# One-hot rows of the gates built for four tokens in four instructions, and six PSUM banks for the first product with the experts

## The chip, the core and the metric

The kernel runs on one core of one Trainium2 chip. The metric is the device time of one execution in microseconds (us). Before the change it is 3218.7 us, the median of 3 runs (3213.13 to 3223.79).

## What is computed

Two small networks stand one behind the other over 256 tokens of width 1024. The first has two layers, each a mixer (retention, then a gated spatial unit) followed by a layer of 16384 experts; the second has forgetting attention, a gated delta rule and two convolutional feed-forward layers. The change touches the expert layer alone, which runs twice:

```python
def peer_ffn(h, w_query, sub_keys, expert_u, expert_v):
    q = (ht @ w_query).reshape(T, Hh, 2, PEER_HALF)
    scores = jnp.einsum('thpd,hpkd->thpk', q, sub_keys)
    s_top, i_top = lax.top_k(scores, K)
    cand = (s_top[:, :, 0, :, None] + s_top[:, :, 1, None, :]).reshape(T, Hh, K * K)
    cand_idx = (i_top[:, :, 0, :, None] * PEER_NKEYS + i_top[:, :, 1, None, :]).reshape(T, Hh, K * K)
    best, pos = lax.top_k(cand, K)
    expert_idx = jnp.take_along_axis(cand_idx, pos, axis=-1)
    gates = jax.nn.softmax(best, axis=-1)
...
        a = jax.nn.gelu(jnp.einsum('tkd,td->tk', u, xb)) * g
        return jnp.einsum('tk,tkd->td', a, expert_v[idx])
```

Each token picks 128 experts (8 heads of 16), each named by two indices below 128.

## The kernel before

The kernel gathers nothing. It multiplies all 16384 experts with all tokens, and puts the choice into a dense table of gates, 128 x 128 x 256, in which the experts that a token did not pick are zero. `peer` (line 976) therefore has these stages in each layer: the query projection; the **first product** (loop from line 1016), 128 blocks of 128 experts, each 24 matmuls of 256 columns (`mm3`, lines 402 to 404: three matmuls for one product, because every f32 weight is split into two parts, `whi` and `wlo`); and the second product (`mult`), which multiplies the activated first product by the gates and the second expert table.

Weights come by DMA on SP's queue as `stage` tiles of 16 blocks (1 MB, two buffers), enough for two blocks of experts. `Weights.load` (line 120) splits four blocks at a time, a piece: ScalarE writes `whi` (line 143), then VectorE, or GpSimd for some pieces, subtracts to get `wlo` (line 145). A block of experts needs two pieces. GpSimd takes every second piece while the experts are being picked (`RELIEF`), and every fourth (`RELIEF_G`) once the gates are being built. Up to eight pieces can wait for TensorE in the first of these stretches and four in the second.

After a block's 24 matmuls ScalarE evicts its PSUM bank with a Gelu (line 1023); after every second block the pair goes to DRAM (line 1025, `spill`). These blocks use two PSUM banks in turn, `b0` and `b1` (`begin_banks(2)`, `bank`). `long_bank` gives the two banks `s0` and `s1` to other work, and the second product keeps `b2` to `b5`.

Beside the first product runs `choose` (line 861), a generator that `step` advances between blocks by an account of estimated nanoseconds. It finds the 16 best keys, the 16 best pairs and the softmax, all on VectorE; at lines 931 to 940 it turns places into indices with long bf16 instructions. Then comes the **gate stage** (lines 959 to 973), four tokens at a time, 64 groups. For each token t, `oh` holds three rows of 128 per slot (slots lie on the partitions): a one-hot row of the first index (line 965), and a one-hot row of the second index times the gate, twice, for the gate's f16 value and for its rest (line 967). The rows of 128 key numbers that they are compared with are `line`. Eight matmuls of 128 columns (line 970) turn these into the 128 x 128 gates of four tokens, and ScalarE copies them out (line 972). `oh` has two buffers. VectorE makes 12 instructions for a group.

The order on each engine is that of the program, except where a scheduler moves an instruction ahead of one that it expects to wait. On ScalarE it puts the splitting of weights ahead: the eviction of a block stands behind `whi` of the block four further on, as long as eight pieces can wait, and behind that of the block two further on in the gate stage.

Of the kernel before, what the change touches and what calls it, by code (L numbers as in the profile page):

```python
# [14 lines left out]
HF = mybir.dt.float16  # L15
# [3 lines left out]
ALU = mybir.AluOpType  # L19
# [4 lines left out]
P = 128  # L24
D = 1024
KC = D // P
T = 256
# [25 lines left out]
NK = 128  # L53
# [268 lines left out]
class Kernel:  # L322
# [538 lines left out]
    def choose(self, scores, big, work, chosen, closing):  # L861

        nc = self.nc
        s16 = big.tile([P, 2, 16, TOPK], F32, tag="s16", name="s16")
        ix = big.tile([P, 2, 16, TOPK], U32, tag="ix", name="ix")
        i12 = chosen.tile([P, 2, T], HF, tag="i12", name="i12")
        gp = chosen.tile([P, 2, T], HF, tag="gp", name="gp")
# [7 lines left out]
            nc.vector.tensor_copy(gp[:, 0, ts], tp[:, 2 * P:3 * P])  # L875
            nc.vector.tensor_tensor(gp[:, 1, ts], tp[:, 2 * P:3 * P], gp[:, 0, ts], op=ALU.subtract)

        line = chosen.tile([P, NK], HF, tag="line", name="line")
        self.tc.keep_in_program_order(nc.vector.tensor_copy(line, self.const("iota")))
        for m in range(16):  # L880
            while m not in scores:
                yield -1
# [6 lines left out]
        iota = big.tile([P, TOPK, P], BF, tag="iota16", name="iota16")  # L889
# [3 lines left out]
        for t in range(2):  # L893
# [34 lines left out]
            for u in range(2):  # L928
# [4 lines left out]
                    op=ALU.is_equal)  # L933
                yield 1200
                nc.vector.tensor_tensor(eq, eq, ixb[:, t, u, :, None].to_broadcast([P, TOPK, TOPK, PEER_H]),
                                        op=ALU.mult)
# [22 lines left out]
        for t4 in range(T // 4):  # L959
            ts = slice(4 * t4, 4 * t4 + 4)  # L960
            acc = self.long_bank()
            oh = chosen.tile([P, 4, 3, NK], HF, tag="oh", name="oh", bufs=2)
            for u in range(4):
                t = slice(4 * t4 + u, 4 * t4 + u + 1)
                nc.vector.tensor_scalar(oh[:, u, 0], line, i12[:, 0, t], None, op0=ALU.is_equal)  # L965
                for w in range(2):
                    nc.vector.tensor_scalar(oh[:, u, 1 + w], line, i12[:, 1, t], gp[:, w, t], op0=ALU.is_equal,  # L967
                                            op1=ALU.mult)
                for w in range(2):
                    nc.tensor.matmul(acc[:, u * P:(u + 1) * P], oh[:, u, 0], oh[:, u, 1 + w], start=w == 0,  # L970
                                     stop=w == 1, skip_group_check=True)
            nc.scalar.activation(gates[:, :, ts], acc.rearrange("p (t i) -> p i t", t=4), AF.Copy,
                                 scale=1.0 / GATE_SCALE)
            yield 1400

    def peer(self, layer, later=()):
        nc = self.nc
        with ExitStack() as ctx:
            io = self.pool("peerio", bufs=2, ctx=ctx)
            chosen = self.pool("peersel", ctx=ctx)  # L980
# [27 lines left out]
            w = self.stream(f"peer_query{layer}", KC * 16)  # L1008
# [4 lines left out]
            self.rate = US  # L1013

            w = Weights(self, self.ins[f"peer_u{layer}"], NK * KC)
            for i in range(NK):
                acc = self.bank()[:, :T]
                for k in range(KC):
                    self.mm3(acc, w.tile(i * KC + k), (self.hi[:, k, :T], self.lo[:, k, :T]), k == 0, k == KC - 1)
                self.tick()  # L1020
                if i % 2 == 0:
                    gs = io.tile([P, 2 * T], F32, tag="gs", name="gs").rearrange("p (a b) -> p a b", a=2)
                nc.scalar.activation(gs[:, i % 2], acc, AF.Gelu_apprx_tanh)  # L1023
                if i % 2:
                    nc.scalar.dma_start(spill[i // 2], gs)
                self.step(self.rate)
# [4 lines left out]
            w = Weights(self, self.ins[f"peer_v{layer}"], NK * KC)  # L1031
# [4 lines left out]
            ts = slice(META, L) if layer else slice(0, T)  # L1036
# [6 lines left out]
            for i in range(NK):  # L1043
                if i % 2 == 0:

                    a = (io if i else chosen).tile([P, 2 * T], F32, tag="gs" if i else "oh", name="gs", bufs=2)
                    a = a.rearrange("p (a b) -> p a b", a=2)
# [679 lines left out]
```

## Time and profile before

| | before |
|---|---|
| median of 3 runs | 3218.7 us |
| the profiled execution, its own time | 3223.57 us |
| its span in the trace | 3221.8 us |
| TensorE busy | 3081.6 us (96%) |
| VectorE busy | 2410.0 us (75%) |
| ScalarE busy | 1774.3 us (55%) |
| GpSimd busy | 526.2 us (16%) |
[...]

The profile lists, for one execution, what every engine did and what it waited for. A matmul's recorded duration is its latency, and successive matmuls overlap, so a short pause of TensorE hides inside the busy time; the distance between events that recur once per block of experts is the better measure of its pace. `PEld` is the loading of weights into TensorE, which runs ahead of the matmuls.

### The profile page before, as it was taken

To read this page: it belongs to the slowest core of one execution; us is meant where nothing else is said; L and a number is where in the kernel's file an instruction comes from. 1 tells how busy PE (TensorE), PEld (TensorE's weight loads), DVE (VectorE), ACT (ScalarE), POOL (GpSimd) and SP (SyncE) were. 2 spreads that over 40 slices of the span, in tenths; PEclk is the share of its full clock that TensorE was granted. 3 is DMA by queue.
4 is the path that set the end of the run, shared out by engine and by line. 5 is a ranking of instruction groups with operands and counts; after the bars stand their busy time and mean duration, and the time that the engine had idled before them with its cause. 6 is when DMAs were issued, how large, how long until landed. Compare 5 with 4: busy or idle time off the path is not lost. (4 is left out here: it accounts for less than half of the span.)

```text
span 3221.8 us, 63744 instructions
## 1 busy us (share of the span) xinstructions
PE 3081.6 (96%) x24317; PEld 2932.2 (91%) x24317; DVE 2410.0 (75%) x5694; ACT 1774.3 (55%) x3495; POOL 526.2 (16%) x476
## 2 busy tenths in 40 slices
PE   6999999999999999999999999999999998999998
PEld 5899999999999978999999999999677998898898
DVE  7777979996777687678899877666556965744783
ACT  4566555555555455555555555556456656824763
POOL 1213431110000003234321200000001001133101
PEclk8999999999999999999999999999899999989999
DMA  6655555558777765455555576665323543310453
GB/s 256 243 189 180 198 196 193 187 182 283 260 260 266 269 229 210 157 179 211 188 193 186 203 277 232 234 231 182 110 76 106 197 171 134 118 40 28 145 191 110
DMA packets 119779, 604.14 MB, mean 188 GB/s; under 512 B 14136, under 2 KB 15336, under 8 KB 61488
## 3 DMA queue, kind: packets, MB, share of 16 engines
q1 hardware_dynamic: 98496, 556.84, 48.8%
q10 hardware_dynamic: 19008, 35.72, 3.0%
q0 software_dynamic: 1968, 7.51, 0.7%
q8 instruction: 190, 3.11, 0.4%
q14 instruction: 117, 0.96, 0.1%
HBM read 565.38 MB, written 34.64 MB: 186 GB/s over the span
## 5 line engine op out<-in xcount | busy, mean ns | idle before, releaser
L402 PE MATMUL bank<-hi,whi 128*128 128x256 f32 (+1 forms) x5968 | 1725.4, 289 | 42.0 <-ACT gs L1023 17.5
L404 PE MATMUL bank<-hi,wlo 128*128 128x256 f32 (+1 forms) x5968 | 1707.5, 286 | 32.5 <-DVE wlo L145 30.2
L403 PE MATMUL bank<-lo,whi 128*128 128x256 f32 (+1 forms) x5968 | 1699.3, 285 | 1.2 <-DVE lo L379 1.2
L143 ACT CAST whi<-stage 128x512 fp32r<-128x512 f32 x1780 | 1077.0, 620 | 1051.7 <-PE bank L403 740.5
L145 DVE TENSOR_TENSOR wlo<-stage,whi 128x512 fp32r<-128x512 f32 x1566 | 1084.6, 707 | 468.0 <-ACT whi L143 452.1
L402 PEld LDWEIGHTS bank<-hi,whi 128*128 128x128 f32 x5968 | 1140.5, 191 | 62.1 <-ACT gs L1023 19.0
L404 PEld LDWEIGHTS bank<-hi,wlo 128*128 128x128 f32 x5968 | 1138.0, 191 | 52.2 <-DVE wlo L145 48.8
L403 PEld LDWEIGHTS bank<-lo,whi 128*128 128x128 f32 x5968 | 1139.0, 191 | 4.9 <-DVE lo L379 2.2
L145 POOL TENSOR_TENSOR wlo<-stage,whi 128x512 fp32r<-128x512 f32 x214 | 306.3, 1433 | 725.0 <-ACT whi L143 717.7
L967 DVE TENSOR_SCALAR oh<-line,i,gp 128x128 f16<-128x128 f16 x1024 | 337.5, 372 | 0.0
L403 PE MATMUL bank<-zl,whi 128*128 128x272 f32 (+1 forms) x736 | 211.3, 287 | 1.0 <-DVE zl L379 1.0
L402 PE MATMUL bank<-zh,whi 128*128 128x272 f32 (+1 forms) x736 | 211.7, 288 | 0.0
L404 PE MATMUL bank<-zh,wlo 128*128 128x272 f32 (+1 forms) x736 | 211.2, 287 | 0.0
L965 DVE TENSOR_SCALAR oh<-line,i 128x128 f16<-128x128 f16 x512 | 150.8, 295 | 0.0
L185 POOL TENSOR_TENSOR sqa<-sqa,sq 128x272 f32<-128x272 f32 (+1 forms) x36 | 30.0, 834 | 692.3 <-ACT sq L183 692.3
L403 PEld LDWEIGHTS bank<-zl,whi 128*128 128x128 f32 x736 | 140.2, 190 | 1.8 <-DVE zl L379 1.4
L402 PEld LDWEIGHTS bank<-zh,whi 128*128 128x128 f32 x736 | 140.1, 190 | 0.7 <-issue 0.4
L404 PEld LDWEIGHTS bank<-zh,wlo 128*128 128x128 f32 x736 | 139.8, 190 | 0.2 <-issue 0.2
L1049 DVE TENSOR_TENSOR gs<-gs,gates 128x512 f32<-128x512 f32 x128 | 88.1, 688 | 55.8 <-DMA gs<-spill 55.5
L1023 ACT ACTIVATE gs<-bank 128x256 f32<-128x256 f32 x256 | 96.8, 378 | 8.0 <-PE bank L404 7.9
L379 DVE TENSOR_TENSOR lo<-gs,hi 128x512 fp32r<-128x512 f32 x126 | 86.4, 686 | 0.4
L378 ACT CAST hi<-gs 128x512 fp32r<-128x512 f32 x126 | 77.9, 618 | 15.1 <-DVE gs L1049 15.0
(432 smaller groups left out, 3114.8 us busy)
## 6 DMA issues: line engine op xcount, KB each, us to landing
stage<-in_peer_u SPq DMA_DIRECT2D x128, 1024.0 KB, 4.8
stage<-in_peer_v SPq DMA_DIRECT2D x128, 1024.0 KB, 5.0
adaw<-in_ada_w SPq DMA_DIRECT2D x96, 512.0 KB, 4.9
stage<-in_ffn_up SPq DMA_DIRECT2D x44, 1024.0 KB, 4.8
spill<-gs ACTq DMA_DIRECT2D x128, 256.0 KB, 2.0
gs<-spill SPq DMA_DIRECT2D x128, 256.0 KB, 5.0
stage<-in_ffn_down SPq DMA_DIRECT2D x22, 1024.0 KB, 4.7
stage<-in_peer_query SPq DMA_DIRECT2D x16, 1024.0 KB, 4.8
```

The costliest lines, as they stand in the source:

```text
L143: k.nc.scalar.copy(hi, src)
L145: eng.tensor_tensor(lo, src, hi.bitcast(F32), op=ALU.subtract)
L185: k.nc.gpsimd.tensor_tensor(self.sum, self.sum, sq, op=ALU.add)
L378: self.nc.scalar.copy(hi, src)
L379: self.nc.vector.tensor_tensor(lo, src, hi.bitcast(F32), op=ALU.subtract)
L402: mm(acc, wh, xh, start=first, stop=False, skip_group_check=True)
L403: mm(acc, wh, xl, start=False, stop=False, skip_group_check=True)
L404: mm(acc, wl, xh, start=False, stop=last, skip_group_check=True)
L965: nc.vector.tensor_scalar(oh[:, u, 0], line, i12[:, 0, t], None, op0=ALU.is_equal)
L967: nc.vector.tensor_scalar(oh[:, u, 1 + w], line, i12[:, 1, t], gp[:, w, t], op0=ALU.is_equal, op1=ALU.mult)
L1023: nc.scalar.activation(gs[:, i % 2], acc, AF.Gelu_apprx_tanh)
L1049: nc.vector.tensor_tensor(a, a, self.gates[:, i:i + 2], op=ALU.mult)
```

## The change

The three rows of a token are no longer made token by token. The key numbers are written twice each (`rep`: 0 0 1 1 2 2 ...), and one instruction makes a kind of row for four tokens as two pairs, the two tokens of a pair interleaved: element 2k+b belongs to key k and token b. So there is one comparison for the first index, one for the second, and two multiplications of the latter with the two parts of the gate: four instructions of 512 elements in place of twelve of 128. All four have two tensor operands. The matmuls stay, eight for a group, but read every second f16 of their rows, as weights and as moving operand. `oh` has a fourth row kind; its tile and its two buffers stay in the same place. The first product takes banks `b0` to `b5` in turn, save for the last four blocks, which stay with `b0` and `b1`.

```diff
-        line = chosen.tile([P, NK], HF, tag="line", name="line")
-        self.tc.keep_in_program_order(nc.vector.tensor_copy(line, self.const("iota")))
+        rep = chosen.tile([P, NK, 2], HF, tag="rep", name="rep")
+        self.tc.keep_in_program_order(
+            nc.vector.tensor_copy(rep, self.const("iota")[:, :, None].to_broadcast([P, NK, 2])))
...
-            oh = chosen.tile([P, 4, 3, NK], HF, tag="oh", name="oh", bufs=2)
-            for u in range(4):
-                t = slice(4 * t4 + u, 4 * t4 + u + 1)
-                nc.vector.tensor_scalar(oh[:, u, 0], line, i12[:, 0, t], None, op0=ALU.is_equal)
-                for w in range(2):
-                    nc.vector.tensor_scalar(oh[:, u, 1 + w], line, i12[:, 1, t], gp[:, w, t], op0=ALU.is_equal,
-                                            op1=ALU.mult)
-                for w in range(2):
-                    nc.tensor.matmul(acc[:, u * P:(u + 1) * P], oh[:, u, 0], oh[:, u, 1 + w], start=w == 0,
-                                     stop=w == 1, skip_group_check=True)
+            oh = chosen.tile([P, 4, 2, NK, 2], HF, tag="oh", name="oh", bufs=2)
+            pairs = lambda a: a[:, ts].rearrange("p (a b) -> p a b", b=2)[:, :, None, :].to_broadcast([P, 2, NK, 2])
+            both = rep[:, None].to_broadcast([P, 2, NK, 2])
+            nc.vector.tensor_tensor(oh[:, 0], pairs(i12[:, 0]), both, op=ALU.is_equal)
+            nc.vector.tensor_tensor(oh[:, 3], pairs(i12[:, 1]), both, op=ALU.is_equal)
+            for w in range(2):
+                nc.vector.tensor_tensor(oh[:, 1 + w], oh[:, 3], pairs(gp[:, w]), op=ALU.mult)
+            for u, w in itertools.product(range(4), range(2)):
+                nc.tensor.matmul(acc[:, u * P:(u + 1) * P], oh[:, 0, u // 2, :, u % 2], oh[:, 1 + w, u // 2, :, u % 2],
+                                 start=w == 0, stop=w == 1, skip_group_check=True)
...
+            wide = itertools.cycle(f"b{i}" for i in range(6))
             for i in range(NK):
-                acc = self.bank()[:, :T]
+                acc = (self.bank() if i >= NK - 4 else self.bank(next(wide)))[:, :T]
```

On TensorE, ScalarE, GpSimd and SP every instruction keeps its place; only PSUM banks and line numbers differ. On VectorE the rows of the gates are replaced, and near the end of the picking a few neighbours change places. VectorE in the middle of the gate stage of layer 0, before (numbers tell the tiles apart; `DVE`, `PE`, `Activation` behind "waits" are VectorE itself, TensorE and ScalarE; `wlo` is the split of a piece of weights):

```order
L965 TENSOR_SCALAR oh_6226<-line_3070,i12_3068 128x128 [waits PE_49]
L967 TENSOR_SCALAR oh_6226<-line_3070,i12_3068,gp_3069 128x128 x2
L965 TENSOR_SCALAR oh_6226<-line_3070,i12_3068 128x128
L967 TENSOR_SCALAR oh_6226<-line_3070,i12_3068,gp_3069 128x128 x2
L965 TENSOR_SCALAR oh_6226<-line_3070,i12_3068 128x128
L967 TENSOR_SCALAR oh_6226<-line_3070,i12_3068,gp_3069 128x128
L145 TENSOR_TENSOR wlo_6192<-stage_6154,whi_6191 128x512 [waits PE_49,Activation_49]
L967 TENSOR_SCALAR oh_6226<-line_3070,i12_3068,gp_3069 128x128
L965 TENSOR_SCALAR oh_6226<-line_3070,i12_3068 128x128
L967 TENSOR_SCALAR oh_6226<-line_3070,i12_3068,gp_3069 128x128 x2
```

The same group now:

```order
L967 TENSOR_TENSOR oh_6154<-i12_3068,rep_3070 128x512 [waits PE_49]
L968 TENSOR_TENSOR oh_6154<-i12_3068,rep_3070 128x512
L970 TENSOR_TENSOR oh_6154<-oh_6154,gp_3069 128x512 [waits DVE_49]
L970 TENSOR_TENSOR oh_6154<-oh_6154,gp_3069 128x512
L145 TENSOR_TENSOR wlo_6120<-stage_6082,whi_6119 128x512 [waits PE_49,Activation_49]
L967 TENSOR_TENSOR oh_6206<-i12_3068,rep_3070 128x512 [waits PE_49]
```

Twelve instructions became four, and the split of the weights that stood among them stands behind them. The first of the four still waits for TensorE, which must have read the rows of two groups earlier; the first multiplication waits for the comparison on its own engine.

## Rows read from the trace of the kernel before

**Rows 1.** Busy time by stretch: two of the gate stage, two ahead of it

```profile
core 0: us, PE busy (x) PEld busy (x) DVE busy (x) ACT busy (x) POOL busy (x), PEclk, DMA share, GB/s
469.18:739.34 270.16, 263.33 (x2395) 254.16 (x2393) 261.85 (x866) 150.54 (x299) 52.32 (x39) 1.00 0.54 193
1579.65:1849.65 270.00, 263.05 (x2394) 254.06 (x2393) 261.85 (x866) 150.64 (x299) 52.44 (x39) 1.00 0.55 192
...
369.88:469.18 99.30, 89.61 (x722) 88.65 (x721) 76.74 (x233) 47.67 (x92) 44.05 (x30) 0.95 0.56 199
1492.78:1579.65 86.87, 78.88 (x626) 77.99 (x625) 66.10 (x184) 42.01 (x80) 37.93 (x25) 0.94 0.53 186
```

**Rows 2.** The same view of line 1023: evictions, two more for table loads ahead of the gates

```profile
469.18:739.34 270.16, 29.47 (x78) 1.00 0.54 193
...
369.88:469.18 99.30, 13.96 (x32) 0.95 0.56 199
1492.78:1579.65 86.87, 12.44 (x28) 0.94 0.53 186
```

**Rows 3.** Timeline of ScalarE's queue: start, us, line 1025, one per two blocks

```profile
341.68 0.33 ACTq L1025 DMA_DIRECT2D spill<-gs  x1
347.32 0.33 ACTq L1025 DMA_DIRECT2D spill<-gs  x1
...
495.66 0.33 ACTq L1025 DMA_DIRECT2D spill<-gs  x1
502.34 0.33 ACTq L1025 DMA_DIRECT2D spill<-gs  x1
```

**Rows 4.** Waits of weight loading, layer 0: gate stage, then ahead of it (us, times, longest)

```profile
PEld bank L404 <- DVE wlo L145: 11.4, 23, 0.8
...
PEld bank L402 <- ACT gs L1023: 10.5, 4, 4.1
```

**Rows 5.** Timeline of VectorE: instructions with two tensor operands, alone and beside GpSimd

```profile
440.85 1.78 DVE L145 TENSOR_TENSOR wlo<-stage,whi 128x512 fp32r<-128x512 f32 x1
...
443.68 0.68 DVE L145 TENSOR_TENSOR wlo<-stage,whi 128x512 fp32r<-128x512 f32 x1
...
445.49 0.41 DVE L939 TENSOR_TENSOR eq<-eq 128x512 bf16<-128x512 bf16 x1
445.82 1.22 DVE L935 TENSOR_TENSOR eq<-eq,ixb 128x2048 bf16<-128x2048 bf16 x1
```

**Rows 6.** Gate stage of layer 0: instructions on `oh` (PE, PEld, DVE); line 145 (DVE, POOL)

```profile
469.18:739.34 270.16, 42.03 (x512) 29.19 (x512) 195.84 (x744) 1.00 0.54 193
...
469.18:739.34 270.16, 77.88 (x117) 52.32 (x39) 1.00 0.54 193
```

**Rows 7.** Timeline of TensorE round one group's matmuls

```profile
564.43 0.62 PE L970 MATMUL bank<-oh 128*128 128x128 f16 x8
564.86 0.36 PE L402 MATMUL bank<-hi,whi 128*128 128x256 f32 x1
```

**Rows 8.** Weight loading by line (count, busy, mean ns); a run of f32 matmuls

```profile
L970 PEld LDWEIGHTS <-oh 128*128 128x128 f16 x1024 | 58.4, 98 | 6.7
...
2879.86 2.17 PE L1548 MATMUL bank<-tn,msk 128*128 128x128 f32 x16
```

**Rows 9.** Timeline of one stall: VectorE, ScalarE, TensorE, and the stretch behind it

```profile
399.16 0.68 DVE L145 TENSOR_TENSOR wlo<-stage,whi 128x512 fp32r<-128x512 f32 x1
...
400.70 0.68 DVE L145 TENSOR_TENSOR wlo<-stage,whi 128x512 fp32r<-128x512 f32 x1
...
402.47 1.14 ACT L143 CAST whi<-stage 128x512 fp32r<-128x512 f32 x2 [7.16 <-DMA stage<-in_peer_u]
403.52 0.38 ACT L1023 ACTIVATE gs<-bank 128x256 f32<-128x256 f32 x1
...
403.94 0.58 PE L402 MATMUL bank<-hi,whi 128*128 128x256 f32 x1 [3.87 <-ACT gs L1023]
...
404.00:408.00 4.00, 4.00 (x23) 4.00 (x24) 1.89 (x2) 1.83 (x4) 2.82 (x2) 0.64 0.79 254
```

## Prediction

> **What bounds the kernel now.** I read the share of busy time first, then the two expert layers in stretches, then the pace of their blocks, and last what ended the pauses. TensorE is busy almost throughout, so only places where it loses pace can give time back. In both expert layers there are two such stretches, the gate stage and some 100 us ahead of it. In the gate stage VectorE is busy 261.85 of 270.16 us, with the edges idle, so it is full; ahead of it no engine is, and the granted clock averages 0.95 and 0.94 where it is 1.00 later [rows 1].
>
> The pace shows more than the busy time. Undisturbed, two blocks of experts take 347.32 - 341.68 = 5.64 us; two blocks with two groups of gates between them take 502.34 - 495.66 = 6.68 us [rows 3], so a group costs TensorE (6.68 - 5.64) / 2 = 0.52 us. Its eight matmuls start at 564.43 and the next line at 564.86, 0.43 us [rows 7]; the rest is the restart behind them. The gate stage of layer 0 has 78 evictions, 39 pairs of blocks [rows 2], and 512 small matmuls, 64 groups [rows 6]. Undisturbed it would take 39 x 5.64 + 64 x 0.52 = 220.0 + 33.3 = 253.3 us. It takes 270.16, the same stage of layer 1 270.00 [rows 1]: **16.9 and 16.7 us are lost, 33.6 in all**. The waits name the cause: loading of weights stands for `wlo`, VectorE's split, 23 times in layer 0, each time for under 0.8 us [rows 4].
>
> Ahead of the gates, layer 0 has 30 evictions without the table loads, 15 pairs, in 99.30 us, and layer 1 has 13 pairs in 86.87 us [rows 1, 2]. At 5.64 they need 84.6 and 73.3, so **14.7 and 13.6 us are lost, 28.3 in all**. Here TensorE waits for an eviction: 10.5 us in four waits in layer 0 [rows 4]. The longest is spelled out in the timeline. ScalarE stood 7.16 us for a stage of weights, split it at 402.47, and only then came to the eviction at 403.52 that freed a bank for TensorE at 403.94. Yet VectorE had finished splits at 399.84 and 401.38, which belong to the two blocks that TensorE was about to begin [rows 9]. Weights were there, a bank was not. [...]
>
> **The change, part by part.** *VectorE in the gate stage.* Now `oh` takes 195.84 us in layer 0 and VectorE's splits 77.88 [rows 6], 273.7 together: all of the stage. The four new instructions have 512 f16 elements and two tensor operands. No row shows one with a run of two elements innermost. The nearest is line 935, which repeats runs of eight, 2048 elements in 1.22 us; the plain bf16 sum of line 939 has 512 in 0.41 us [rows 5]. Between the two lie 0.53 ns for an element, so the repetition costs nothing there. From below, they follow each other at 445.82 - 445.49 = 0.33 us; from above, an f32 split of 512 elements takes 0.68 [rows 5]. I take 0.33 to 0.41, since length and size of an element are those of line 939, and line 935 adds the repetition: 256 x that is 84 to 105 us. Beside GpSimd a split took 1.78 in place of 0.68 [rows 5], 1.1 us more; GpSimd has 39 splits here [rows 1], so at most 43 us more. VectorE then needs 84 + 78 = 162 to 105 + 78 + 43 = 226 us, and TensorE 253.3. TensorE becomes the bound, and the waits for `wlo` go.
>
> [...]
>
> *The new wait.* The first comparison of a group waits until TensorE has read the rows of two groups before, and the split of the next block's weights is queued behind it. That release comes two groups ahead, at least 2 x 24 matmuls or 5.64 us before TensorE needs those weights; four instructions of up to 0.41 and two or three splits of 0.68 [rows 5] take 3.0 to 3.7 us. So the wait costs nothing alone. If GpSimd holds up two of them, 2 us of cover are gone as well, and short waits remain: I leave 2 us in each layer, and take 29 of the 33.6 us. Bounds: none of it, or all.
>
> *TensorE's matmuls.* They keep their number and now read elements 4 bytes apart. Bounds: no change, or the rate of f32 operands, whose elements lie as far apart. The f32 run of line 1548 has 16 matmuls in 2.17 us, or (2.17 - 0.28) / 15 = 0.126 us each [rows 8], against 0.43 / 8 = 0.054 now: 0.58 us more for a group. I take no change, because f32 matmuls of 256 columns run at 5.64 / 48 = 0.118 us [rows 3], as many columns per us as these, so distance alone does not slow the moving side. The weights are the open point: f16 ones load in 98 ns [rows 8], and no f16 load with gaps is in the trace.
>
> [...]
>
> *The six banks.* They remove the wait for an eviction. In ScalarE's order an eviction stands behind the weights of the block four further on, so with a bank at hand TensorE can go on with two more blocks that are already split, 5.64 us, where the longest wait was 4.1 [rows 4]. What comes next is the stage that landed at 402.47: its first piece takes ScalarE half of the 1.14 us that two took, and VectorE 0.68 behind it, so it is ready at about 403.8 [rows 9]. The pause began at 403.94 - 3.87 = 400.07; two blocks later is 405.7. That is in time by almost 2 us, and the low clock behind the pause goes too. I take 24 of the 28.3 us; bounds none (the wait passes to `whi`) and all. ScalarE, GpSimd and SP keep their order, and in the gate stage evictions were not waited for. Writing `rep` in place of `line`, twice in the program, lies in VectorE's gaps.
>
> *Sum.* 29 + 24 = 53 us. The profiled execution took 3223.57 us, which is 4.9 above the median of 3218.7, so I put the new median at 3218.7 - 53 = **3166 us**.
>
> **Rivals.** *The banks do not help* because weights are short as well. For it: four waits follow times when VectorE and GpSimd were crowded. Against it: the two splits that lay ready. Only the 29 us come: 3190.
>
> *The comparisons run at the f32 rate.* At 0.68 they take 256 x 0.68 = 174 us, VectorE 252 to 295 with the same splits and hindrance; in the middle, 274, it is as full as now and the gate stage gives nothing. Then 3218.7 - 24 = 3195, and at the upper end, 295, some 25 us more for each layer, 3245.
>
> *The operands with gaps are slow.* This one ends slower than before. At 0.126 us for each matmul a group costs 0.58 us more, the gate stage becomes TensorE's at 253.3 + 64 x 0.58 = 290 us instead of 270, 40 us for both layers, less the banks' 24: 3235. All gains are used up at 53 / 128 = 0.41 more for a group, 0.105 us for each matmul; at 0.115 it is 0.3% slower. For it: f32 weights load at this pace. Against it: the type.
>
> **Chances.** About 0.3%, 10 us, is what a measurement of this kernel can tell from no change. The forecast 0.70, banks without effect 0.10, slow comparisons 0.08, slow operands 0.12. Faster: 0.70 + 0.10 + 0.05 of the slow comparisons = 0.85. The same: 0.03 of these and 0.04 of the slow operands, 0.07. Slower: the remaining 0.08. The range: all 62 us from the lowest run, 3213 - 62 = 3151, so 3150 below; above, both middle rivals, 3195, and the profiled execution's 4.9 us and a little more, 3204. What lies outside is the slow operands and half of the slow comparisons' spread, under 0.2.
>
> **What would show it.** In the gate stage: 39 pairs in about 255 us, 6.68 us where two groups lie between, VectorE idle for over 40 us, the four instructions at about 0.41 us each, and no waits for `wlo` worth counting. Ahead of it: no wait for line 1027, the eviction's new number, no interval near 10 us between pairs, a clock of 1.00. Eight gate matmuls within 0.43 us. I am wrong if the four take about 0.7 us, if the eight take more than 0.8, or if waits for `whi` or `wlo` stand where those for evictions stood.

## The result and the profile after

The change takes 3174.0 us, the median of four runs (3167.5 to 3179.4), against 3216.9 before (four runs): a ratio of 0.9866, with a 95% interval of 0.9847 to 0.9884. It is 42.9 us faster; the forecast was 53, and 3174 lies in its range. The profiled execution took 3167.53 us with a span of 3165.8.

The four stretches again, with the columns of [rows 1], in the windows of the changed kernel:

```profile
core 0: us, PE busy (x) PEld busy (x) DVE busy (x) ACT busy (x) POOL busy (x), PEclk, DMA share, GB/s
368.66:460.94 92.28, 86.59 (x722) 86.18 (x721) 74.74 (x221) 45.34 (x92) 46.52 (x29) 0.98 0.58 210
460.94:716.93 255.99, 255.99 (x2394) 253.27 (x2393) 202.89 (x370) 150.77 (x299) 53.62 (x40) 1.00 0.57 203
1470.66:1551.29 80.63, 77.02 (x645) 76.22 (x644) 63.46 (x168) 39.52 (x80) 40.86 (x25) 1.00 0.56 202
1551.29:1805.02 253.73, 253.73 (x2374) 251.00 (x2373) 202.83 (x370) 150.31 (x299) 53.96 (x40) 1.00 0.57 205
```

The two gate stages (second and fourth line) went from 270.16 and 270.00 to 255.99 and 253.73 us. TensorE is busy for the whole of both, and VectorE, full before, is free for a fifth of them. The stretches ahead of them went from 99.30 and 86.87 to 92.28 and 80.63. That makes 14.2 + 16.3 + 7.0 + 6.2 = 43.7 us, within 1 us of the difference of the medians.

The border between the two stretches needs care in layer 1. It is a transfer of ScalarE's queue, and in the change it came late against TensorE: 645 matmuls lie ahead of it, 626 in [rows 1]. At 5.64 / 48 = 0.118 us each the 19 more are 2.2 us, which belong to the stretch ahead. Counted by TensorE's work, the gate stages gained 14.2 and 14.0 us, 28.2 together, and the stretches ahead of them 7.0 and 8.5, 15.5 together.

The two profiled executions differ by 56.0 us; the other 12 lie outside these stretches, where the change touches nothing, most of them behind the second gate stage. That part takes from 1361 to 1374 us in the profiles of this document, in no order with the kernels, and before's profiled execution was 6.7 us above its median, this one 6.5 below; so I put those 12 us down to spread between runs.

**The gate stage.** The same window, instructions on `oh` (PE, PEld, DVE), then line 145 (DVE, POOL), as in [rows 6]:

```profile
460.94:716.93 255.99, 40.50 (x512) 29.46 (x512) 128.13 (x248) 1.00 0.57 203
...
460.94:716.93 255.99, 80.37 (x117) 53.62 (x40) 1.00 0.57 203
```

VectorE's work on the gates' rows fell from 195.84 to 128.13 us, and with splits it needs 208.5 of the 255.99. The instructions by line (min/median/max in ns, then first and last start):

```profile
L967 DVE TENSOR_TENSOR oh<-i,rep x128: 404/421/814, 425.1 to 1786.0; 128x512 f16<-128x512 f16 x128
...
L968 DVE TENSOR_TENSOR oh<-i,rep x128: 408/422/1525, 427.4 to 1786.3; 128x512 f16<-128x512 f16 x128
...
L970 DVE TENSOR_TENSOR oh<-oh,gp x256: 400/422/1401, 427.9 to 1788.2; 128x512 f16<-128x512 f16 x128
...
L972 PEld LDWEIGHTS <-oh x1024: 95/97/101, 463.4 to 1795.3; 128*128 128x128 f16 x171
```

Alone, each of the four takes 0.42 us, about the 0.41 of line 939 in [rows 5]. The last line is the load of weights 4 bytes apart: 97 ns, where packed ones took 98 [rows 8]. TensorE's timeline round one group's matmuls, as [rows 7]:

```profile
562.37 0.63 PE L972 MATMUL bank<-oh 128*128 128x128 f16 x8
562.81 0.36 PE L402 MATMUL bank<-hi,whi 128*128 128x256 f32 x1
```

The eight take 0.44 us instead of 0.43. Nobody waits for `wlo` in the gate stage any more: loading of weights and matmuls have no wait in it. VectorE's own waits there, line waited for, us, times, longest:

```profile
DVE wlo L145 <- ACT whi L143: 33.0, 53, 2.8
...
DVE oh L967 <- PE bank L972: 17.2, 31, 0.7
```

The second is the wait that the change added: VectorE stands 17.2 us until TensorE has read older rows, and it costs nothing, because TensorE never stands still.

The pace, line 1029 being the transfer behind every second block (line 1025 before), two groups in the first interval and one in the second:

```profile
560.07 0.33 ACTq L1029 DMA_DIRECT2D spill<-gs  x1
566.80 0.33 ACTq L1029 DMA_DIRECT2D spill<-gs  x1
573.01 0.33 ACTq L1029 DMA_DIRECT2D spill<-gs  x1
```

6.73 and 6.21 us. Reckoned as in the prediction, a group now costs TensorE (6.73 - 5.64) / 2 = 0.545 us, where it was 0.52.

**Ahead of the gates.** Waits of weight loading, layer 0, then layer 1:

```profile
PEld bank L404 <- DVE wlo L145: 6.1, 2, 4.2
...
PEld bank L404 <- DVE wlo L145: 3.8, 3, 1.9
PEld bank L404 <- POOL wlo L145: 0.7, 1, 0.7
```

The 10.5 us of waits for an eviction in layer 0 [rows 4] are gone, and waits for `wlo` stand in their place. The first and the longest, in the timelines of VectorE, ScalarE, GpSimd and TensorE, with the stretch behind the longest (columns of the windows):

```profile
395.08 0.39 PE L404 MATMUL bank<-hi,wlo 128*128 128x256 f32 x1 [1.70 <-DVE wlo L145]
...
401.38 1.14 ACT L143 CAST whi<-stage 128x512 fp32r<-128x512 f32 x2 [10.19 <-DMA stage<-in_peer_u]
...
431.38 6.06 POOL L145 TENSOR_TENSOR wlo<-stage,whi 128x512 fp32r<-128x512 f32 x4 [6.97 <-ACT whi L143]
...
431.83 1.28 DVE L948 TENSOR_SCALAR den<-den 128x8 f32<-128x8 f32 x1
...
433.68 1.36 DVE L926 CAST place<-ab 128x256 bf16<-128x256 f32 x1
434.97 1.46 DVE L950 TENSOR_TENSOR nat<-g,den 128x128 f32<-128x128 f32 x1
436.26 2.26 DVE L932 TENSOR_TENSOR eq<-place,iota 128x2048 bf16<-128x2048 bf16 x1
...
438.45 0.68 DVE L145 TENSOR_TENSOR wlo<-stage,whi 128x512 fp32r<-128x512 f32 x1
...
439.18 0.39 PE L404 MATMUL bank<-hi,wlo 128*128 128x256 f32 x1 [4.00 <-DVE wlo L145]
...
440.00:444.00 4.00, 4.00 (x25) 4.00 (x25) 4.00 (x7) 0.00 (x0) 0.00 (x0) 0.64 0.74 262
```

TensorE stands 4.00 us for a split on VectorE, at 438.45, that stands behind instructions of the picking. The one at 436.26 begins beside GpSimd's splits and takes 2.26 us; line 935 with the same length took 1.22 alone [rows 5]. The three shown ahead of it are drawn out too: lines 948, 926 and 950 take 0.16, 0.40 and 0.41 us in this trace where GpSimd is idle (at 400.16, 386.10 and 400.59). Together the four lost 4.2 us beside four splits on GpSimd, about as long as TensorE then stood. Behind the pause the granted clock is 0.64 over 4 us, as it was before [rows 9].

### The profile page after: what moved, and what is told of

It reads as the page before. It is cut to its first block, busy times and chain, and to the rows that moved or that the text cites. A ratio compares the mean times of both kernels' runs of the same rounds, so it can differ in the third digit from the quotient of the medians.

```text
span 3165.8 us, 62716 instructions
## 1 busy us (share of the span) xinstructions
PE 3053.3 (96%) x24317; PEld 2919.9 (92%) x24317; DVE 2288.7 (72%) x4670; ACT 1766.4 (56%) x3495; POOL 533.5 (17%) x476
## 5 line engine op out<-in xcount | busy, mean ns | idle before, releaser
L145 POOL TENSOR_TENSOR wlo<-stage,whi 128x512 fp32r<-128x512 f32 x214 | 313.5, 1469 | 672.4 <-ACT whi L143 641.8
L968 DVE TENSOR_TENSOR oh<-i,rep 128x512 f16<-128x512 f16 x128 | 119.6, 934 | 0.0
L970 DVE TENSOR_TENSOR oh<-oh,gp 128x512 f16<-128x512 f16 x256 | 98.5, 425 | 4.2
```

The lines of the kernel that those rows point to most:

```text
L145: eng.tensor_tensor(lo, src, hi.bitcast(F32), op=ALU.subtract)
L968: nc.vector.tensor_tensor(oh[:, 3], pairs(i12[:, 1]), both, op=ALU.is_equal)
L970: nc.vector.tensor_tensor(oh[:, 1 + w], oh[:, 3], pairs(gp[:, w]), op=ALU.mult)
```

## The experiments

All times are medians in us. The stretches are measured between the same transfers of line 1029 as above (its number differs in before, e2, e3 and e11), in each run's profiled execution, one for each kernel; the change and its repeat e8 differ by 2 us in one of them. Where a gate stage reads below 255.9, the transfer at its start came late as in layer 1 of the change, and what is missing lies in the stretch ahead. The runs of before that stand beside each kernel had medians of 3216.9 to 3222.3.

| kernel | ahead, layers 0 / 1 | gate stage, 0 / 1 | median | ratio to before (95%) |
|---|---|---|---|---|
| before | 99.30 / 86.87 | 270.16 / 270.00 | 3216.9 | |
| the change | 92.28 / 80.63 | 255.99 / 253.73 | 3174.0 | 0.9866 (0.9847 to 0.9884) |
| e1 rows only | 101.47 / 91.31 | 255.98 / 256.00 | 3187.6 | 0.9907 (0.9880 to 0.9935) |
| e2 banks only | 95.64 / 81.77 | 269.93 / 269.45 | 3204.9 | 0.9964 (0.9948 to 0.9980) |
| e3 plain rows | 93.69 / 81.98 | 277.17 / 276.69 | 3216.6 | 0.9994 (0.9974 to 1.0014) |
| e4 four banks | 93.73 / 80.07 | 255.98 / 255.30 | 3176.8 | 0.9861 (0.9834 to 0.9889) |
| e5 more pieces | 91.19 / 81.09 | 254.91 / 255.45 | 3181.0 | 0.9897 (0.9857 to 0.9937) |
| e6 fewer on GpSimd | 88.64 / 77.61 | 255.41 / 253.97 | 3160.5 | 0.9829 (0.9791 to 0.9866) |
| e7 none on GpSimd | 84.54 / 73.77 | 255.98 / 256.00 | 3158.5 | 0.9813 (0.9776 to 0.9851) |
| e8 the change again | 90.21 / 80.11 | 255.66 / 254.43 | 3178.0 | 0.9885 (0.9844 to 0.9925) |
| e9 e1 and e7 together | 91.71 / 78.18 | 255.98 / 256.00 | 3168.8 | 0.9842 (0.9822 to 0.9863) |
| e10 e7, none in the gates | 85.26 / 73.77 | 255.93 / 255.95 | 3161.4 | 0.9828 (0.9805 to 0.9851) |
| e11 before, none on GpSimd | 89.78 / 77.00 | 270.12 / 270.44 | 3194.3 | 0.9925 (0.9896 to 0.9954) |

### The parts apart: e1 and e2

e1 keeps the new rows and goes back to two banks:

```diff
-                acc = (self.bank() if i >= NK - 4 else self.bank(next(wide)))[:, :T]
+                acc = self.bank()[:, :T]
```

> The rows of the gates as in the change, the first product back on two banks. Theory (two gains that add up: VectorE leaves the bound in the gate stage, and spare banks bridge late evictions ahead of it): the gate stages take about 250 us in place of 270 each, with 6.73 us for two blocks and two groups, and the stretch ahead of them keeps its waits for evictions, about 10 us in each layer, and its length of 99 and 87 us; so about 42 of the profiles' 56 us come, near 3177, ratio 0.987. Rival (the banks do nothing of their own, the rows are all of it): the whole gain, 3174 with waits for evictions as small as in the changed kernel. Rival (the banks were worth the 24 us forecast and the rows less): 3190 or more.

Measured: 0.9907, some 30 us faster than before; the median of 3187.6 is some 10 us above the 3177 expected. The gate stages are those of the change; ahead of them nothing is gained, and the waits for evictions are back, in layer 0 (in all, then the end of the last one):

```profile
PEld bank L402 <- ACT gs L1027: 12.2, 4, 4.8
...
460.78 0.39 PE L402 MATMUL bank<-hi,whi 128*128 128x256 f32 x1 [2.52 <-ACT gs L1027]
```

The stage's length in the expectation was read one pair of blocks too early; between the same two transfers it is 255.99 us. That these stretches are 2 and 4 us longer than before is not explained. The wait at 460.78 is one that before does not have at that block; a few of VectorE's instructions changed places near the end of the picking, and no run isolates them. Part of it may be spread: e1's profiled execution, 3200.4 us, was 12.7 above its median.

e2 has the banks and the old rows:

```diff
+            wide = itertools.cycle(f"b{i}" for i in range(6))
...
-                acc = self.bank()[:, :T]
+                acc = (self.bank() if i >= NK - 4 else self.bank(next(wide)))[:, :T]
```

> Six banks for the first product, the rows of the gates as before. Theory: the waits for evictions go and in part come back as waits for wlo, the stretch ahead of the gates gets 6 to 7 us shorter in each layer, the gate stage stays at 270 us; about 13 us in all, 3204, ratio 0.996. Forecast of the prediction: 24 us, 3193, ratio 0.9925. Rival (weights are short as well): no change, 3217.

Measured: 0.9964, some 12 us faster, gate stages as before; ahead of them its profile is 3.7 and 5.1 us shorter, less than the 6 to 7 expected. Its waits ahead of them in layer 0:

```profile
PEld bank L404 <- DVE wlo L145: 8.2, 3, 4.3
```

The banks alone turn waits for evictions into waits for `wlo`, with the old rows just as with the new ones. Parts and sum agree: by the ratios 30 + 12 = 42 us, the change 42.9. The intervals are wide, 21 to 39 us for e1 and 6 to 17 for e2.

### What the interleaving is worth: e3

The same four instructions and 512 elements, but rows of 128 packed, so that the token's number is one element read 128 times:

```diff
-            oh = chosen.tile([P, 4, 2, NK, 2], HF, tag="oh", name="oh", bufs=2)
-            pairs = lambda a: a[:, ts].rearrange("p (a b) -> p a b", b=2)[:, :, None, :].to_broadcast([P, 2, NK, 2])
-            both = rep[:, None].to_broadcast([P, 2, NK, 2])
+            oh = chosen.tile([P, 4, 4, NK], HF, tag="oh", name="oh", bufs=2)
+            each = lambda a: a[:, ts][:, :, None].to_broadcast([P, 4, NK])
+            keys = line[:, None].to_broadcast([P, 4, NK])
...
-                nc.tensor.matmul(acc[:, u * P:(u + 1) * P], oh[:, 0, u // 2, :, u % 2], oh[:, 1 + w, u // 2, :, u % 2],
+                nc.tensor.matmul(acc[:, u * P:(u + 1) * P], oh[:, 0, u], oh[:, 1 + w, u],
```

> The changed kernel, but the four instructions write each token's row by itself: the index of a token is read 128 times in a row, so the innermost step of one operand is 0, and the matmuls read packed f16. Theory (the pairs are what gives the doubled pace): the four instructions take about 0.69 us each in place of 0.42, VectorE needs 161 to 177 us for the rows, 78 for its splits and some 40 for GpSimd's hindrance, 280 to 295 in a gate stage, and is the bound again: 10 to 25 us more than the 270 of before in each layer, less 13 of the banks, so 3225 to 3255, ratio 1.003 to 1.012. Rival (an innermost step of 0 costs nothing, the gain is that of fewer instructions): 0.42 us, 3174, ratio 0.987. On TensorE: if elements 4 bytes apart cost anything there, eight gate matmuls take less here than the 0.44 us of the changed kernel; the theory says the same 0.43 to 0.44.

Measured: 0.9994, not to be told from before; the loss of 0.3 to 1.2% that was expected did not come. Line 967 of this kernel by duration, then its gate stage in layer 0 (columns of the windows), the instructions on `oh` in it, its waits, and two transfers of undisturbed blocks with two groups between them:

```profile
L967 DVE TENSOR_TENSOR oh<-i,line x128: 676/683/1789, 428.8 to 1831.3; 128x512 f16<-128x512 f16 x128
...
462.06:739.23 277.17, 261.06 (x2397) 253.59 (x2396) 267.23 (x370) 151.01 (x299) 57.95 (x39) 1.00 0.52 188
...
462.06:739.23 277.17, 41.27 (x512) 29.30 (x512) 192.17 (x248) 1.00 0.52 188
...
PEld bank L404 <- DVE wlo L145: 13.2, 14, 1.2
...
481.83 0.33 ACTq L1028 DMA_DIRECT2D spill<-gs  x1
...
488.51 0.33 ACTq L1028 DMA_DIRECT2D spill<-gs  x1
```

The comparison takes 0.68 us in place of 0.42, VectorE's rows take 192.17 us in place of 128.13, and it is full again, 267.23 of 277.17. The gate stages are 7.0 and 6.7 us longer than before, which uses up the 5.6 and 4.9 us that the banks give ahead of them. So the gain of the gate stage does not come from fewer instructions, which e3 has as well: it hangs on the pair innermost. TensorE, whose operands are packed here, does the eight matmuls of a group in 0.43 us, as before, and two blocks with two groups in 488.51 - 481.83 = 6.68 us; the change needs 0.44 and 6.73. So the steps of the change seem to cost TensorE some 0.025 us a group, 3 us for the 128 groups of both layers.

### How many banks, and a longer stock: e4 and e5

e4 has four banks for the first product:

```diff
-            wide = itertools.cycle(f"b{i}" for i in range(6))
+            wide = itertools.cycle(f"b{i}" for i in range(4))
```

> The changed kernel with four banks in turn in place of six. Theory (an eviction stands behind the weights of the block four further on, so two blocks beyond the two that two banks allow are ready, and the rest is weights): no different from six, 3174, ratio 0.987, no waits for evictions. Rival (banks five and six matter): waits for evictions come back, 3177 to 3187.

Measured: 0.9861, as six banks, with the same kind of wait ahead of the gates in layer 0:

```profile
PEld bank L404 <- DVE wlo L145: 6.0, 2, 4.0
```

No wait for an eviction is left with four, so the fifth and sixth bank are worth nothing that was measured.

e5 leaves the banks and lengthens the stock of pieces of weights:

```diff
-WR, WS, WA, WF, WD, WP = 2, 2, 4, 8, 2, 4
+WR, WS, WA, WF, WD, WP = 2, 2, 4, 8, 2, 6
```

> The changed kernel with ten split pieces of weights that can wait for TensorE while experts are picked, in place of eight. What is left ahead of the gates are waits for wlo, 6.1 us in layer 0 and 4.5 in layer 1 with the low clock behind them, 7 us lost in each. Theory (the split that TensorE waits for stands behind the long bf16 instructions on VectorE, and a longer stock bridges it): the waits shrink to under 2 us in each layer, the stretch gets 4 to 6 us shorter in each, 3162 to 3166. Rival (VectorE and GpSimd are short over the whole burst, or the two stages of weights are the limit): within 3 us of the changed kernel.

Measured: 0.9897, 3181.0 us where 3162 to 3166 were expected, with an interval that overlaps those of the change and its repeat. The waits in layer 0 are about as long as in the change, in layer 1 longer (7.4 us in three, 4.5 in four in the change):

```profile
PEld bank L404 <- DVE wlo L145: 5.4, 2, 4.6
...
PEld bank L404 <- DVE wlo L145: 7.4, 3, 5.5
```

So a longer stock of pieces gave nothing that was measured.

### GpSimd beside VectorE: e6, e7, e8, e10

`RELIEF` says which of the splits go to GpSimd during the picking: every second, every fourth (e6), none (e7).

```diff
-RELIEF = 2
+RELIEF = 4
```

> The changed kernel with every fourth piece on GpSimd while experts are picked, in place of every second. Theory (VectorE and GpSimd hold each other up, about 1 us for each split of GpSimd that falls on an instruction with two operands, which is more than the 0.62 us of VectorE's time that GpSimd spares): the long instructions run at 1.2 us more often than at 2.3, waits for wlo shrink, 3 to 5 us less in each layer, 3164 to 3168. Rival (VectorE has too much to do there): it gets slower, 3176 to 3185, with more waits for wlo.

Measured: 0.9829, 3160.5 us, and ahead of the gates 88.64 and 77.61 us. Waits in layer 0:

```profile
PEld bank L404 <- DVE wlo L145: 3.4, 3, 1.4
```

```diff
-RELIEF = 2
+RELIEF = 0
```

> The changed kernel with no split on GpSimd while experts are picked. Theory as for every fourth piece, further on: no instruction of VectorE is held up there, the long ones take 1.2 us throughout; VectorE gets some 16 splits more than with every fourth, 10 us, in a stretch of 90 us in which it is busy for 75 now, of which some 25 are hindrance: 3164 to 3172. Rival (VectorE has too much to do): 3180 to 3200, with VectorE full ahead of the gates and waits for wlo.

Measured: 0.9813, 3158.5 us. Its stretches ahead of the gates, with the columns of the windows:

```profile
368.78:453.32 84.54, 84.54 (x722) 84.54 (x721) 77.29 (x257) 45.34 (x92) 1.28 (x1) 1.00 0.66 231
1459.40:1533.17 73.77, 73.77 (x626) 73.77 (x625) 65.97 (x201) 39.89 (x80) 1.30 (x1) 1.00 0.65 228
```

TensorE is busy throughout at a granted clock of 1.00, and 84.54 and 73.77 us are what 15 and 13 pairs need undisturbed at 5.64. VectorE, which has taken over 28 of GpSimd's 29 splits in layer 0, is busy only 77.29 - 74.74 = 2.55 us longer than in the change, with 36 instructions more. The long instruction of the picking by line, first in the change, then in e7:

```profile
L932 DVE TENSOR_TENSOR eq<-place,iota x8: 1210/2263/2345, 386.5 to 1529.8; 128x2048 bf16<-128x2048 bf16 x8
```

```profile
L932 DVE TENSOR_TENSOR eq<-place,iota x8: 1208/1220/1226, 389.1 to 1512.1; 128x2048 bf16<-128x2048 bf16 x8
```

The median of the eight is 2.26 us beside GpSimd; without it none takes over 1.23. That GpSimd's own splits come too late would be another reading of e7; but of the 10.6 us of waits that the change has left in both layers, 0.7 are for a split on GpSimd.

e8 is the change once more, beside e5 to e7 on their chip:

> The changed kernel once more, beside the three others on the same chip. Both theories: 3174 within 4 us, ratio 0.985 to 0.989.

Measured: 0.9885, 3178.0 us, with an interval (0.9844 to 0.9925) that holds the first result. e6 and e7 have lower ones beside it: all four runs of each (at most 3166.2) lie below the fastest of e8 (3166.3), and both medians lie below the 3164 at which the expectations' ranges began.

e10 takes GpSimd off in the gate stage as well:

```diff
-RELIEF = 2
-RELIEF_G = 4
+RELIEF = 0
+RELIEF_G = 0
```

> No split on GpSimd in the gate stage either. Theory (TensorE bounds the gate stage now): VectorE has 39 splits more there, 24 us, and loses the hindrance, some 35 us, so it stays below TensorE and the stage takes 254 to 256 us as before, 3158 within 3 us. Rival (VectorE's queue is close to the limit in the gate stage): waits for wlo in it, 260 us or more in each layer, 3168 or more.

Measured: 0.9828, no better than e7, and gate stages of 255.93 and 255.95: TensorE is the bound there, so VectorE's hindrance costs nothing. But it is gone; line 968 by duration, whose longest was 1525 ns in the change, and the instructions on `oh` in the gate stage of layer 0:

```profile
L968 DVE TENSOR_TENSOR oh<-i,rep x128: 404/419/429, 421.6 to 1771.6; 128x512 f16<-128x512 f16 x128
...
451.36:707.29 255.93, 40.50 (x512) 29.48 (x512) 93.96 (x248) 1.00 0.58 204
```

VectorE's rows take 93.96 us in place of 128.13.

### Are the banks needed at all: e9 and e11

e9 is e1 with `RELIEF` at 0, two banks:

```diff
-                acc = (self.bank() if i >= NK - 4 else self.bank(next(wide)))[:, :T]
+                acc = self.bank()[:, :T]
...
-RELIEF = 2
+RELIEF = 0
```

> Four-instruction rows, two banks, and no split on GpSimd while experts are picked. Theory (evictions came late because ScalarE stood for a stage of weights that VectorE and GpSimd, holding each other up, had not released; spare banks only bridge that): without the cause two banks lose little, the short waits behind ScalarE's table loads, 1 to 3 us in each layer: 3160 to 3165, ratio 0.981 to 0.983. Rival (two banks are too few in themselves): the waits for evictions stay near 10 us in each layer, 3172 or more.

Measured: 0.9842, 3168.8 us, between the theory's 3165 and the rival's 3172. Waits for evictions remain, layer 0 and layer 1, then the longest of them in the timelines of ScalarE and TensorE:

```profile
PEld bank L402 <- ACT gs L1027: 4.4, 2, 4.0
...
PEld bank L402 <- ACT gs L1027: 4.3, 2, 2.2
...
382.37 0.62 ACT L143 CAST whi<-stage 128x512 fp32r<-128x512 f32 x1 [4.66 <-DVE pos L859]
383.01 1.28 ACT L945 ACT_TABLE_LOAD   x1
...
384.63 1.28 ACT L1027 ACT_TABLE_LOAD   x1
...
386.36 0.58 PE L402 MATMUL bank<-hi,whi 128*128 128x256 f32 x1 [3.83 <-ACT gs L1027]
```

The eviction that TensorE waits for stands behind two table loads of 1.28 us, one for the exponential of the picking and one for the Gelu behind it, and ScalarE came to these late, after standing for 4.66 us. Against e7 the stretches ahead of the gates are 7.2 and 4.4 us longer. Most of what was lost with two banks came from GpSimd, but not all.

e11 is the kernel before with that one constant:

```diff
-RELIEF = 2
+RELIEF = 0
```

> The kernel before, with no split on GpSimd while experts are picked and nothing else changed. Theory: the stretch ahead of the gates gets 10 to 13 us shorter in each layer, the gate stage keeps its 270 us: 3194 to 3200, ratio 0.992 to 0.994, as much as or more than the six banks gave by themselves. Rival (two banks are too few in themselves): under 5 us.

Measured: 0.9925, 24 us faster than before with old rows and two banks, more than the 12 that the banks alone gave; in the profiles it is 9.5 and 9.9 us ahead of the gates, against 3.7 and 5.1. So the stretch ahead of the gates had two causes, and the change took away only one.

## Why the prediction was right, and where it was off

**The gate stage: right in kind, and in size partly by luck.** 29 us were forecast, 14.2 + 14.0 = 28.2 measured, and e1 by itself gave some 30. The steps hold one by one. VectorE's rows and splits need 128.13 + 80.37 = 208.5 us, inside the 162 to 226. The four instructions take 0.42 us, just above the 0.33 to 0.41. TensorE becomes the bound, and the waits for `wlo` there are gone. VectorE has 255.99 - 202.89 = 53 us free; "over 40" was forecast. The new wait costs nothing, and operands with gaps cost next to nothing, with the load of weights at 97 ns.

The luck lies in the 29. They were 33.6 less 4.6 for short waits behind GpSimd, and these waits did not come. What is missing instead is TensorE's own time: 255.99 us is 2.7 more than the 253.3 reckoned, with no wait in it, so a group costs (255.99 - 220.0) / 64 = 0.56 us and not 0.52. The gaps explain some 0.025 of that; the rest stays open.

The rival of slow comparisons fell with 0.42 us. e3 shows its price: at 0.68 the gate stages get 7 us longer each, and 3216.6 lies between this rival's 3195 and its upper end of 3245.

The rival of slow operands fell as well: the load of weights 4 bytes apart took 97 ns where packed ones took 98 [rows 8], and a group's eight matmuls 0.44 us where they took 0.43 [rows 7].

**Ahead of the gates: right in kind, the size was off.** 24 us were forecast, 7.0 + 8.5 = 15.5 measured, and e2 alone gave some 12. The failed step is "What comes next": it took one stage of weights in one pause, found it "in time by almost 2 us", and let that stand for the whole stretch. That stage was in time: ScalarE splits it at 401.38 in the change, and TensorE does not wait for it. But TensorE, no longer held up for banks, now came to other splits before they were done: at 395.08, for a piece of the stage before, it stood 1.70 us, and at 439.18 it stood 4.00 us, with a granted clock of 0.64 behind it, for a split that a hindered VectorE had not begun. "The low clock behind the pause goes too", a clock of 0.64 before [rows 9], fell with that, and what the prediction named as a sign of being wrong, waits for `wlo` where those for evictions stood, came true here. The first rival, weights short as well, held for a third to a half of this term. The hindrance was in the working, as 1.1 us for a split beside GpSimd [rows 5], but charged only to the gate stage, where there turned out to be room for it; ahead of the gates it was left out. e7 shows its price: with banks and without GpSimd's splits all of the 28 us come back, 99.30 to 84.54 and 86.87 to 73.77. With all of that the change would have given 28.2 + 27.9 = 56 us, a little more than the forecast; e7's ratio gives 60, with an interval of 48 to 72.

**What stays open:** why e1 is slower ahead of the gates than the kernel before, and what else makes a group cost TensorE 0.56 us.

The lowest median is that of e7, the change with no splits on GpSimd during the picking, 0.9813 of before; e6 and e10 cannot be told from it.

## What to carry to other kernels

Measure a stretch by an event that comes once per unit of work, and compare the undisturbed pace with the real one: this gave the gate stage to within 3 us a layer, where busy shares alone say only that an engine is full. When a wait is to be removed, work out what is late next at every pause of the stretch, with each engine's durations as they are beside its neighbours, not alone. And a helper engine is to be priced by what it does to the engine it helps: here the cheapest 24 us were one constant that takes work away from it.

## What the runs showed of the hardware

Instructions of VectorE took longer beside splits on GpSimd, many of them by about 1.1 us, short ones as well as long ones: 0.68 became 1.78 us for a split [rows 5], 1.22 became 2.26 for line 932, 0.42 became up to 1.53 for line 968, 0.16 became 1.28 for line 948. That is 1.04 to 1.12 us each, half more than the 0.68 that VectorE needs to do such a split itself. Others lost less: line 967 took 0.81 at most in place of 0.42. In the gate stage of layer 0 the rows take 128.13 us beside 40 splits on GpSimd and 93.96 without, 0.85 us for each on average, since not every one meets a row: 30 instructions of line 968 take 1.51 or 1.52 us there. GpSimd pays too: four splits take 6.06 us, 1.5 each, where the one left in e7 takes 1.28. It is not only instructions with two tensor operands that are held up, as the expectation of e6 had it: line 948 has one.
